# Two tiles on another engine, one buffer more and other planning numbers in a two-layer decoder kernel

## The chip, the core and the metric

The kernel runs on one core of a Trainium2 chip. The metric is device time of one execution in microseconds (us). The time before is 2131.61 us, the median of three runs (2131.43 to 2131.8).

## What is computed

Two layers on x of 1024 tokens by 1024 features, in float32. Layer 0 mixes tokens with a Conformer convolution, layer 1 with sliding-window attention. Each layer then has a layer norm on a scaled residual, a squared-ReLU MLP of inner width 4096, a second norm, and a gated per-layer embedding. Cut to what matters here:

```python
def conformer_conv(x, ...):
    h = x @ w_in + b_in
    a, gate = jnp.split(h, 2, axis=-1)
    h = a * jax.nn.sigmoid(gate)
    h = depthwise_conv(h, w_dw) + b_dw          # 31 taps, causal
    h = jax.nn.silu(layer_norm(h, ln_g, ln_b))
    return h @ w_out + b_out

def swa_sink_attention(x, ...):                 # 16 query heads, 4 key heads, blocks of 128
    scores = where(mask, q @ k / 8, -inf)       # a block sees itself and the block before
    lse = logaddexp(logsumexp(scores), sink)
    return (exp(scores - lse) @ v) @ w_o

def sq_relu_mlp(x, w_up, w_down):
    return jnp.square(jax.nn.relu(x @ w_up)) @ w_down
```

## The kernel before

Each float32 operand is split in two fp32r parts (`wh` and `wl` for weights, `xTh` and `xTl` for the transposed activations), and a product is three matmuls: high by high, high by low, low by high. Larger products use seven half-size products instead of eight, with sums and differences of operands formed on VectorE. PSUM tiles are called `ps` and `tr`.

The order of the work isn't the order of the code. A recorder notes every operation, and a list scheduler (`Recorder.schedule`) then writes one order for all engines: it keeps a planned clock for each engine, takes the duration of each operation from `cost()` (L302) and the planned landing time of a DMA from the table `LANDING` (L87, in ns, by tile name), and issues what can begin first by its rules. A number in these tables therefore moves instructions on every engine and takes no time itself. All instructions come out of one helper, so all stand at line L480 in the profile; tiles have to be told apart by name.

Four places matter here.

- **The convolution's end (taps, 225 to 262 us).** The taps are matmuls `ps<-z,E` of 128x256. Their spread weights `E` are formed on VectorE from `B` (`E<-B,E`), and VectorE also adds tap results together (`A<-A,ps`) and copies transposed pieces out (`A<-tr`). Results go to a DRAM tile `zd` and come back as token rows, `X` (the first 512 features) and `A` (the other 512), as soon as all of a column is written (`X<-zd`, `A<-zd` on SyncE's queue). `conv_ln` (L924) takes BN_STATS of these on VectorE as they land.
- **The norm and what follows (262 to 290 us).** For each half h of the tokens `conv_ln` computes scale and shift (`sm`, with a power on GpSimd), normalises four `X` tiles and four `A` tiles, has TensorE transpose them in groups of four, applies SiLU on ScalarE (`z<-tr` or `z<-ps`), casts the result to `xTh` on ScalarE or VectorE, and forms `xTl` from both on VectorE. `NORM[h][q][f]` (L44) says which engine normalises tile f of X (q = 0) or A (q = 1): v VectorE, a ScalarE, g GpSimd. `CAST[h]` (L45) lists the feature blocks whose cast to `xTh` is ScalarE's; the others are VectorE's. The matmuls of `mix_out` (`ps<-wh,xTh` and so on) wait for these. Matmuls of an embedding projection (`ps<-wh,wh`) are there to fill.
- **The MLP's inner activations.** `mlp()` (L1237) makes the four quarters of a pair of inner tiles; `keep()` (L1076) then forms four sums of them on VectorE, s1 to s4, and stores each to the DRAM tile `hid` by SyncE. s1 and s2 are the two halves of one `zz` tile (one slot), s3 takes the place of a quarter, and s4 is written over s2, once s2's store has read it. `head_forms()` (L1098) does the same for the pairs that were made ahead; both are called after the third pair (m = `HEAD_FORMS` = 2). Later the down product loads these sums back (`wh<-hid`, `raw<-hid`).
- **Attention (1178 to 1345 us).** For each block of 128 queries and four heads, TensorE makes scores (`ps<-E,X`), ScalarE copies one half of them to a `z` tile (`z<-ps`) and VectorE the other by a mask (`COPY_PREDICATED z<-cst,ps`); VectorE takes the negative maximum, ScalarE four exponentials with their sums, VectorE the reciprocal, and GpSimd multiplies each head by it (`TENSOR_SCALAR z<-z,sm`, 128x128). TensorE transposes the four (`ps<-ident,z`), ScalarE and VectorE split them in `A` tiles, GpSimd masks copies of these (`AFFINE_SELECT A<-A`), and TensorE multiplies by the values (`tr<-A,v`, `tr<-A,bo`). Query and output projections fill the gaps.

Of the kernel before, what the change touches and what calls it, by code (L numbers as in the profile page):

```python
# [13 lines left out]
ALU = mybir.AluOpType  # L14
# [7 lines left out]
HT = 512  # L22
# [7 lines left out]
NFF = 4 * D // P  # L30
# [10 lines left out]
LO = 288  # L41
LAG = 8
EMBEDDED = 2
NORM = (("vavg", "vgvg"), ("vgvg", "gggg"))  # L44
CAST = (1, 3, 5, 7), (1, 3, 5, 7)  # L45
DIRECT = 5
BACK = (7, 0, 1)
PLAIN = 2
# [19 lines left out]
HEAD_FORMS, SUMS, FIRST, DEFER = 2, (4, 6), 8, 300  # L68
# [15 lines left out]
    },  # L84
)
CST = 256 + 2 * NH
LANDING = dict(scr=4000.0, qd=5000.0, kd=5000.0, ad=5500.0, zd=4500.0, wsum=5000.0, proj=4500.0, xsp=4000.0, hid=3400.0)  # L87
SLACK = 900.0
LOADED = 1500.0

# [120 lines left out]
class Recorder:  # L211
# [90 lines left out]
    def cost(self, o, outs, allv):  # L302
        e, n = o.eng, o.name
        f = outs[0].n if outs and isinstance(outs[0], View) else 1024
        if e == "tensor":
            if n == "transpose":
                return 113.5
            return f * 0.4427
        if n == "dma_start":
            return 920.0 if e == "gpsimd" else 620.0 if any(v.buf.tag in ("qd", "kd") for v in allv) else 420.0  # L310
        if e == "scalar":
            t = 60.0 + f * 0.85
            if n == "activation":
                t += sum(c for k, c in (("bias", 90.0), ("scale", 130.0), ("accum_out", 110.0)) if isinstance(o.kw.get(k), View))
            return t
        if e == "gpsimd":
            if n == "tensor_tensor":
                return 590.0 if o.kw["op"] == ALU.pow else 60.0 + 3.1 * f
            return 100.0 + 1.95 * f if n == "tensor_scalar" else 160.0 + 0.95 * f
        psum = any(v.buf.space == "PSUM" for v in allv)  # L320
        if n == "tensor_scalar" and not psum:
            return 100.0 + f * 0.69
        if n in ("bn_stats", "tensor_reduce"):
            return 69.0 + 1.042 * allv[-1].n
        if n == "reciprocal":
            return 60.0 + 6.3 * f
        t = 120.0 if isinstance(o.kw.get("scalar"), View) else 70.0
        return t + f * 1.042

    def schedule(self):  # L330
# [45 lines left out]
        def finish(o, end):  # L376
            o.end = end
            order.append(o)
            for x in o.outs:
                r = end + delay(o, x) + (0.0 if o.eng in ("tensor", "alloc") else x.slack)  # L380
                if r > x.ready:
                    x.ready = r
                x.left -= 1
                if x.left == 0:
                    enable(x)
            for b in o.bufs:
                b.users -= 1
                b.end = max(b.end, end)
                if b.users == 0 and b.slot is not None:
                    heapq.heappush(self.tags[b.tag]["free"], (b.end + lat, b.slot))  # L390
                    serve(b.tag)
# [24 lines left out]
        while True:  # L416
# [41 lines left out]
            if o.name == "dma_start":  # L458
                v = o.allv[0]
                dma = max(dma, t + 1400.0) + v.n * v.parts / 75.0  # L460
                names = [x.buf.tag.rstrip("0123456789_") for x in o.allv]
                least = max(LANDING.get(x, 2800.0) for x in names)
                finish(o, max(dma, t + (6500.0 if e == "gpsimd" else least)))
# [49 lines left out]
class Emit:  # L513
# [200 lines left out]
    def conv(self):  # L714
# [209 lines left out]
        def conv_ln(h):  # L924
# [13 lines left out]
            for q in range(2):  # L938
                for f in range(PH):
                    z = Z[h, f, q]  # L940
                    if NORM[h][q][f] == "a":
                        nc.scalar.activation(z, z, AF.Identity, bias=rs[:, f, 1:2], scale=rs[:, f, 0:1])
                        continue
                    e = {"v": nc.vector, "g": nc.gpsimd}[NORM[h][q][f]]
                    e.tensor_scalar(out=z, in0=z, scalar1=rs[:, f, 0:1], scalar2=rs[:, f, 1:2], op0=ALU.mult, op1=ALU.add)
            for k in range(KB):
# [4 lines left out]
                sl = (slice(None), k, slice(h * HT, (h + 1) * HT))  # L951
                if k in CAST[h]:
                    nc.scalar.copy(self.xTh[sl], sv)
# [122 lines left out]
    def keep(self, i, f, c, new=True):  # L1076

        nc = self.nc
        sub, add = ALU.subtract, ALU.add
        w = nc.tile("zz", (P, 1024), F32)  # L1080
        s1, s2 = w[:, 0:HT], w[:, HT : 2 * HT]
        nc.vector.tensor_tensor(out=s1, in0=c[0, 1], in1=c[1, 1], op=add)
        self.store(i, f, "s1", s1)
        if new:
            self.store(i, f, (1, 1), c[1, 1])
        nc.vector.tensor_tensor(out=s2, in0=s1, in1=c[0, 0], op=sub)
        self.store(i, f, "s2", s2)
        s3 = c[0, 1]
        nc.vector.tensor_tensor(out=s3, in0=c[0, 0], in1=s3, op=sub)
        self.store(i, f, "s3", s3)  # L1090
        if new:
            self.store(i, f, (0, 0), c[0, 0])
        nc.vector.tensor_tensor(out=s2, in0=c[1, 0], in1=s2, op=sub)
        self.store(i, f, "s4", s2)
        if new:
            self.store(i, f, (1, 0), c[1, 0])

# [139 lines left out]
    def mlp(self, i):  # L1237
        nc, d, ws = self.nc, self.d, self.ws
        tags, xtags = (dict(zip((2, 1, 3, 4), "XAEB")), "EB") if i == 0 else (dict(zip((2, 1, 3, 4), "XEAB")), "AB")
        first, pairs = list(range(HEAD[i])), list(range(HEAD[i], NFF, 2))  # L1240
        ws.add(*[d["w_up"][i, f] for f in first])
        for f in pairs:
            ws.add(*self.pair_units([d["w_up"][i, f + k] for k in range(2)]))

        us = ws.get(len(first))
        for h in range(2):
            for f in first:
                self.store(i, f, (f % 2, h), self.up(f, h, us[f]))
        ws.done(len(first))

        T = self.token_forms(tags)
        plain = {
            (a, h): [tuple(x[:, k + 4 * a, h * HT : (h + 1) * HT] for x in (self.xTh, self.xTl)) for k in range(4)]
            for a, h in ((0, 0), (1, 0), (1, 1))
        }

        prod = self.half_product

        def copy(ps, tag="t"):
            v = self.sb(tag)  # L1260
            nc.scalar.copy(v, ps)
            return v

        def plus(a, ps):
            nc.vector.tensor_tensor(out=a, in0=a, in1=ps, op=ALU.add)
            return a


        for m, f in enumerate(pairs):
            w = ws.get(1)[0]  # L1270
            p = prod(w, 0, plain[0, 0])
            c11 = copy(p)
            p2 = prod(w, 1, plain[1, 0])
            ws.done(1)
            w12 = ws.get(1)[0]
            prod(w12, 0, T[2], p)
            c21 = copy(p)
            self.square(plus(c11, p2), "z")
            w34 = ws.get(1)[0]
            r = prod(w34, 0, T[3])  # L1280
            prod(w12, 1, T[1], p)
            ws.done(1)
            c22 = copy(p, "bo")
            self.square(plus(c22, r), "z")
            w = ws.get(1)[0]
            prod(w34, 1, plain[1, 1], p)
            c12 = self.square(p, "z")
            prod(w, 0, T[4], r)
            ws.done(2)
            self.square(plus(c21, r), "z")  # L1290
            with nc.later(DEFER if f == pairs[-1] else 0):
                self.keep(i, f, {(0, 0): c11, (0, 1): c12, (1, 0): c21, (1, 1): c22})
            if m == HEAD_FORMS:
                for g in first[::2]:
                    self.head_forms(i, g)
            if m in SUMS:
                self.down_sums(i, SUMS.index(m))
            if f == NFF - FIRST:
                ops = self.first_operands(i)

        self.x = []
        for t in range(NT):
            self.x.append(self.pair(xtags[t // 4]))
        self.begun = set()
        self.turn = 0
        for k in range(3):
            nc.move("tr", "ps")
        for n, cs in enumerate(DOWN):
            self.down_seven(i, cs, None if n else ops, n == len(DOWN) - 1)
# [650 lines left out]
```

## Time and profile before

| | |
|---|---|
| median of three runs | 2131.61 us (2131.43 to 2131.8) |
| profiled execution, time | 2130.39 us |
| its span on the core | 2128.7 us |
| around the span (2130.39 - 2128.7) | 1.7 us |
| granted TensorE clock | 0.999 |
| busy: PE, DVE, ACT, POOL | 99%, 73%, 49%, 10% |

In the profile PE is TensorE, DVE VectorE, ACT ScalarE, POOL GpSimd, SP SyncE. A timeline row has the start in us, the duration in us, the engine, the operation with out<-in, the shape, a count of merged instructions (the duration then runs from the first start to the last end), and in square brackets the idle time just before and what ended it. Matmuls are pipelined, so that the durations of neighbours overlap; the step from start to start says what a matmul costs.

### The profile page before, as it was taken

To read this page: it belongs to the slowest core of one execution; us is meant where nothing else is said; L and a number is where in the kernel's file an instruction comes from. 1 tells how busy PE (TensorE), PEld (TensorE's weight loads), DVE (VectorE), ACT (ScalarE), POOL (GpSimd) and SP (SyncE) were. 2 spreads that over 40 slices of the span, in tenths; PEclk is the share of its full clock that TensorE was granted. 3 is DMA by queue.
4 is the path that set the end of the run, shared out by engine and by line. 5 is a ranking of instruction groups with operands and counts; after the bars stand their busy time and mean duration, and the time that the engine had idled before them with its cause. 6 is when DMAs were issued, how large, how long until landed. Compare 5 with 4: busy or idle time off the path is not lost.

```text
span 2128.7 us, 28513 instructions
## 1 busy us (share of the span) xinstructions
PE 2116.5 (99%) x10067; PEld 1762.7 (83%) x10067; DVE 1562.8 (73%) x2362; ACT 1044.3 (49%) x1886; POOL 206.9 (10%) x390
## 2 busy tenths in 40 slices
PE   9999999999999999999999999999999999999999
PEld 7888888888888888888889877888888888888887
DVE  8766868966666787889554798796665658878993
ACT  7555743555555433341323798365555563333321
POOL 0000141000000200000000566100000011000010
PEclk9999999999999999999999999999999999999999
DMA  7679882347547955530567671354654598445223
GB/s 248 194 205 281 276 216 99 105 168 241 180 167 295 252 183 174 175 127 25 170 193 221 212 234 60 114 195 147 214 197 139 182 332 241 152 159 188 90 70 104
DMA packets 208078, 384.61 MB, mean 181 GB/s; under 512 B 28736, under 2 KB 82496, under 8 KB 207936
## 3 DMA queue, kind: packets, MB, share of 16 engines
q1 hardware_dynamic: 200880, 369.96, 52.2%
q0 software_dynamic: 6912, 12.59, 3.4%
q8 instruction: 79, 1.29, 0.3%
q14 instruction: 63, 0.52, 0.1%
q10 hardware_dynamic: 144, 0.26, 0.0%
HBM read 263.98 MB, written 114.56 MB: 178 GB/s over the span
## 4 chain that ended last, share of the span: by engine, by line
PE 93%; DVE 3%; DMA 1%; ACT 1%; issue 0%; POOL 0%; SPq 0%; DVEq 0%; ACTq 0%; POOLq 0%
PE ps L480 71%; PE tr L480 21%; DMA wh<-hid 1%; DVE xTl L480 1%; DVE sm L480 0%; ACT z L480 0%; DVE wl L480 0%; DVE E L480 0%; DVE B L480 0%; DVE A L480 0%; DVE t L480 0%; DVE z L480 0%; DMA X<-qd 0%; POOL A L480 0%; ACT t L480 0%
## 5 line engine op out<-in xcount | busy, mean ns | idle before, releaser
L480 DVE TENSOR_TENSOR wl<-raw,wh 128x1024 fp32r<-128x1024 f32 (+2 forms) x144 | 151.5, 1053 | 132.8 <-ACT wh L480 132.2
L480 PE MATMUL ps<-xTl,xTh 128*128 128x512 f32 x628 | 244.3, 389 | 0.0
L480 PE MATMUL ps<-xTh,xTl 128*128 128x512 f32 x628 | 244.3, 389 | 0.0
L480 PE MATMUL ps<-xTh 128*128 128x512 f32 x628 | 244.1, 389 | 0.0
L480 PE MATMUL ps<-xTh,wh 128*128 128x512 f32 x608 | 238.8, 393 | 1.1 <-ACT bo L480 0.5
L480 PE MATMUL ps<-xTl,wh 128*128 128x512 f32 x608 | 238.5, 392 | 0.0
L480 PE MATMUL ps<-xTh,wl 128*128 128x512 f32 x608 | 237.6, 391 | 0.0
L480 ACT CAST wh<-raw 128x1024 fp32r<-128x1024 f32 (+2 forms) x144 | 131.2, 913 | 195.7 <-PE ps L480 93.7
L480 DVE TENSOR_TENSOR wl<-g,wh 128x512 fp32r<-128x512 f32 x140 | 92.1, 687 | 97.3 <-ACT wh L480 97.2
L480 PE MATMUL ps<-wl,xTh 128*128 128x512 f32 (+1 forms) x424 | 162.6, 384 | 0.0
L480 PE MATMUL ps<-wh,xTh 128*128 128x512 f32 (+1 forms) x424 | 161.5, 383 | 0.0
L480 PE MATMUL ps<-wh,xTl 128*128 128x512 f32 (+1 forms) x424 | 160.6, 380 | 0.0
L480 ACT CAST wh<-g 128x512 fp32r<-128x512 f32 x140 | 82.8, 621 | 143.7 <-PE ps L480 89.4
L480 ACT CAST xTh<-wh 128x1024 fp32r<-128x1024 f32 x78 | 81.9, 1050 | 126.4 <-PE ps L480 100.6
L480 PEld LDWEIGHTS ps<-xTh,xTl 128*128 128x128 f32 x628 | 117.8, 188 | 24.6
L480 PEld LDWEIGHTS ps<-xTh 128*128 128x128 f32 x628 | 117.9, 188 | 24.5
L480 PEld LDWEIGHTS ps<-xTl,xTh 128*128 128x128 f32 x628 | 117.9, 188 | 24.4
L480 PEld LDWEIGHTS ps<-xTh,wh 128*128 128x128 f32 x608 | 114.3, 188 | 26.7 <-ACT bo L480 1.5
L480 PEld LDWEIGHTS ps<-xTh,wl 128*128 128x128 f32 x608 | 114.4, 188 | 23.5
L480 PEld LDWEIGHTS ps<-xTl,wh 128*128 128x128 f32 x608 | 114.5, 188 | 21.9 <-DVE xTl L480 0.2
L480 DVE TENSOR_TENSOR xTl<-wh,xTh 128x1024 fp32r<-128x1024 f32 x78 | 95.3, 1222 | 27.8 <-ACT xTh L480 27.8
L480 DVE TENSOR_TENSOR xTl<-wl,xTh 128x1024 fp32r<-128x1024 f32 x80 | 97.4, 1220 | 3.7 <-ACT xTh L480 3.7
(316 smaller groups left out, 4962.2 us busy)
## 6 DMA issues: line engine op xcount, KB each, us to landing
wh<-hid SPq DMA_DIRECT2D x80, 512.0 KB, 4.5
raw<-in_w_up_dram SPq DMA_DIRECT2D x64, 512.0 KB, 4.0
wl<-in_w_down_dram SPq DMA_DIRECT2D x60, 512.0 KB, 4.6
hid<-zz SPq DMA_DIRECT2D x96, 256.0 KB, 3.2
hid<-t SPq DMA_DIRECT2D x70, 256.0 KB, 2.7
raw<-hid SPq DMA_DIRECT2D x30, 512.0 KB, 4.5
z<-scr SPq DMA_DIRECT2D x32, 256.0 KB, 3.5
proj<-t SPq DMA_DIRECT2D x32, 256.0 KB, 3.6
```

The costliest lines, as they stand in the source:

```text
L480: getattr(getattr(nc, o.eng), o.name)(*a, **k)
```

## The change

It has six edits.

1. In half 0 the second `A` tile that GpSimd normalised goes to ScalarE (`NORM`, L44).
2. In half 0 the casts to `xTh` on ScalarE are those of blocks 0, 1, 2, 4, 6 in place of 1, 3, 5, 7 (`CAST`, L45).
3. The planned landing time of transfers with `zd` goes from 4500 to 6500 ns, with `hid` from 3400 to 4500 ns (`LANDING`, L87).
4. GpSimd's planned durations change (`cost()`): a power 590 to 560; a tensor_tensor of f elements 60 + 3.1f to 90 + 2.2f; a tensor_scalar of fewer than 512 elements 100 + 1.95f to 160 + 1.17f; the rest 160 + 0.95f to 160 + 1.17f.
5. In `keep()` s4 gets a buffer of its own (a fresh `t` tile; for the pairs made ahead it is written over quarter (1, 0), which isn't needed any longer; for the last pairs over s1) in place of s2's half of `zz`.
6. `head_forms()` is called for one pair after the third pair and for the other after the fourth.

```diff
-NORM = (("vavg", "vgvg"), ("vgvg", "gggg"))
-CAST = (1, 3, 5, 7), (1, 3, 5, 7)
+NORM = (("vavg", "vavg"), ("vgvg", "gggg"))
+CAST = (0, 1, 2, 4, 6), (1, 3, 5, 7)
...
-LANDING = dict(scr=4000.0, qd=5000.0, kd=5000.0, ad=5500.0, zd=4500.0, wsum=5000.0, proj=4500.0, xsp=4000.0, hid=3400.0)
+LANDING = dict(scr=4000.0, qd=5000.0, kd=5000.0, ad=5500.0, zd=6500.0, wsum=5000.0, proj=4500.0, xsp=4000.0, hid=4500.0)
...
             if n == "tensor_tensor":
-                return 590.0 if o.kw["op"] == ALU.pow else 60.0 + 3.1 * f
-            return 100.0 + 1.95 * f if n == "tensor_scalar" else 160.0 + 0.95 * f
+                return 560.0 if o.kw["op"] == ALU.pow else 90.0 + 2.2 * f
+            return 100.0 + 1.95 * f if n == "tensor_scalar" and f >= HT else 160.0 + 1.17 * f
...
-        s3 = c[0, 1]
+        s3, s4 = c[0, 1], c[1, 0] if not new else s1 if f >= NFF - 4 else self.sb("t")
...
-        nc.vector.tensor_tensor(out=s2, in0=c[1, 0], in1=s2, op=sub)
-        self.store(i, f, "s4", s2)
+        nc.vector.tensor_tensor(out=s4, in0=c[1, 0], in1=s2, op=sub)
+        self.store(i, f, "s4", s4)
...
-            if m == HEAD_FORMS:
-                for g in first[::2]:
-                    self.head_forms(i, g)
+            if 0 <= m - HEAD_FORMS < len(first) // 2:
+                self.head_forms(i, first[2 * (m - HEAD_FORMS)])
```

TensorE's order is the same in both programs but for three places: at the end of the taps, between the norm and the output projection of layer 0, and in attention. Three pieces follow.

First, VectorE at the end of the taps. `X_589`, `X_600`, `X_602`, `X_604` and `X_609` are token rows loaded from `zd`; `A_678` and `A_692` are sums of tap results, `E_684` to `E_690` spread weights. Before:

```order
L480 TENSOR_TENSOR A_678_2797<-A_678_2797,ps_657_2682 64x512
L480 TENSOR_TENSOR E_684_2843<-B_653_2658,E_684_2843 128x9x64
L480 BN_STATS sm_64_128<-X_602_2400 128x6
L480 TENSOR_TENSOR E_687_2861<-B_655_2670,E_687_2861 128x9x64
L480 TENSOR_TENSOR E_690_2879<-B_661_2701,E_690_2879 128x9x64
L480 COPY A_579_2312<-tr_670_2765 128x64
L480 BN_STATS sm_65_129<-X_604_2406 128x6
L480 COPY A_594_2372<-tr_670_2765 128x64
L480 BN_STATS sm_68_132<-X_609_2437 128x6
L480 TENSOR_TENSOR A_692_2891<-A_692_2891,ps_680_2815 64x512
```

After the change:

```order
L480 BN_STATS sm_62_126<-X_589_2356 128x6
L480 TENSOR_TENSOR E_687_2859<-B_655_2670,E_687_2859 128x9x64
L480 COPY A_579_2312<-tr_670_2765 128x64
L480 TENSOR_TENSOR E_690_2877<-B_661_2701,E_690_2877 128x9x64
L480 COPY A_594_2372<-tr_670_2765 128x64
L480 BN_STATS sm_63_127<-X_600_2393 128x6
L480 TENSOR_TENSOR A_692_2887<-A_692_2887,ps_680_2815 64x512
```

The statistics have moved back: the sum `A_692`, which frees a PSUM bank, now stands behind those of two X tiles, where it stood behind those of five.

Second, VectorE between the norm's last tiles of half 0 and its first `xTl`. `z_688` is the first SiLU result, `sm_67` the scale and shift of half 1, `X_609` and `X_620` are X tiles of half 1. Before:

```order
L480 TENSOR_TENSOR wl_629_2521<-raw_617_2478,wh_628_2519 128x1024
L480 TENSOR_TENSOR wl_705_2960<-raw_630_2524,wh_706_2964 128x1024
L480 CAST xTh_340<-z_688_2862 128x512
L480 CAST xTh_340<-z_711_2985 128x512
L480 TENSOR_TENSOR xTl_341<-z_688_2862,xTh_340 128x512
L480 TENSOR_TENSOR xTl_341<-z_697_2915,xTh_340 128x512
```

After the change:

```order
L480 TENSOR_TENSOR wl_629_2521<-raw_617_2478,wh_628_2519 128x1024
L480 SCALAR_TENSOR_TENSOR sm_67_131<-sm_66_130,sm_67_131 128x4
L480 TENSOR_TENSOR wl_705_2959<-raw_630_2524,wh_706_2962 128x1024
L480 TENSOR_SCALAR X_609_2437<-X_609_2437,sm_67_131 128x512
L480 TENSOR_SCALAR X_620_2491<-X_620_2491,sm_67_131 128x512
L480 TENSOR_TENSOR xTl_341<-z_688_2860,xTh_340 128x512
L480 TENSOR_TENSOR xTl_341<-z_696_2913,xTh_340 128x512
```

The two casts are gone from here, to ScalarE, and two tiles of half 1 have come in ahead of the first `xTl`.

Third, ScalarE at the same place; `A_592` is the tile that came from GpSimd. After the change:

```order
L480 ACTIVATE X_600_2393<-X_600_2393,sm_61_125 128x512
L480 ACTIVATE A_592_2366<-A_592_2366,sm_61_125 128x512
L480 CAST wh_628_2519<-raw_617_2478 128x1024
L480 CAST wh_706_2962<-raw_630_2524 128x1024
L480 ACTIVATE z_688_2860<-tr_713_3014,cst_337 128x512
L480 ACTIVATE z_696_2913<-ps_722_3068,cst_337 128x512
L480 CAST xTh_340<-z_688_2860 128x512
```

Before, the second of these rows wasn't there, and a third SiLU (`z_711`) stood where the cast of `z_688` stands now. On TensorE the transposes of half 1's X tiles stand earlier than before.

## Prediction

> **What bounds the kernel now.** First the engines' busy share on the page, then TensorE's waits over the whole span, then TensorE's share by stage.
>
> ```profile
> PE 2116.5 (99%) x10067; PEld 1762.7 (83%) x10067; DVE 1562.8 (73%) x2362; ACT 1044.3 (49%) x1886; POOL 206.9 (10%) x390
> ```
>
> ```profile
> PE ps L480 <- DVE t L480: 1.5, 1, 1.5
> PE ps L480 <- POOL z L480: 1.2, 2, 0.7
> PE ps L480 <- DVE z L480: 1.0, 2, 0.8
> PE ps L480 <- issue: 1.0, 1, 1.0
> PE ps L480 <- POOL A L480: 0.8, 1, 0.8
> PE tr L480 <- DVE t L480: 0.7, 3, 0.3
> PE ps L480 <- ACT bo L480: 0.5, 1, 0.5
> PE ps L480 <- ACT xTh L480: 0.5, 1, 0.5
> PE tr L480 <- DVE B L480: 0.2, 1, 0.2
> ```
>
> ```profile
> 310.00:1178.00 868.00, 867.30 (x4020) 722.24 (x4019) 619.27 (x877) 374.59 (x568) 38.99 (x59) 1.00 0.53 173
> 1178.00:1345.00 167.00, 163.81 (x868) 132.01 (x867) 141.75 (x295) 133.28 (x453) 100.62 (x216) 1.00 0.55 172
> 1345.00:2128.70 783.70, 779.29 (x3519) 645.27 (x3518) 570.86 (x809) 348.58 (x520) 31.25 (x48) 1.00 0.50 168
> 800.00:900.00 100.00, 100.00 (x443) 82.81 (x442) 80.02 (x96) 35.49 (x40) 0.00 (x0) 1.00 0.53 174
> ```
>
> In the stage rows the columns are length, busy time of PE, PEld, DVE, ACT, POOL, PE's clock, DMA share, GB/s. TensorE is the bound, at full clock, and its named waits add up to 7.4 us, 1.5 of them at the start. The change adds and removes no matmul. So it can win only what is left of these waits, and lose wherever a reordered helper comes late. From 310 to 1178 TensorE idles 0.7 of 868 us, both of the MLP's products of layer 0 included. The last row gives the unit: 100 us / 443 = 0.226 us per 128x512 matmul. A measurement of this kernel can tell 0.2%, or 4.3 us, from no change.
>
> **Taps (longer `zd` loads).** TensorE's longest wait of this stage, and VectorE's rows that lead to its end; then the load.
>
> ```profile
> 247.48 0.71 PE L480 MATMUL ps<-z,E 128*128 128x256 f32 x4 [1.02 <-issue]
> ```
>
> ```profile
> 240.21 0.69 DVE L480 BATCH_NORM_STATS2 sm<-X 128x6 f32<-128x512 f32 x1 [1.47 <-DMA X<-zd]
> ...
> 243.06 0.69 DVE L480 BATCH_NORM_STATS2 sm<-X 128x6 f32<-128x512 f32 x1
> ...
> 245.97 0.68 DVE L480 BATCH_NORM_STATS2 sm<-X 128x6 f32<-128x512 f32 x1
> 246.69 0.69 DVE L480 TENSOR_TENSOR A<-A,ps 64x512 f32<-64x512 f32 x1
> ```
>
> ```profile
> X<-zd SPq DMA_DIRECT2D x8, 256.0 KB, 6.3
> ```
>
> The matmul at 247.48 needs the bank that the sum at 246.69 frees at 247.38. The sum was late because VectorE stood 1.47 us for a token load that took 6.3 us where 4.5 were planned, and had five statistics of 0.69 ahead of it. With 6.5 planned three of them move behind the sum. Walking VectorE's new order with these durations, the bank is free at about 245.5. But TensorE comes there four matmuls sooner (four of the filling matmuls now stand behind): its own unhindered time is the wait's start 247.48 - 1.02 = 246.46, less 4 x 0.226, so about 245.5. The wait shrinks to 0.1: **gain 0.9**. Bounds: all of it, 1.0; or, if the release stays at 247.38, the four matmuls of cover lost, 0.9 slower.
>
> **Norm (edits 1 and 2).** TensorE, GpSimd (its A tiles by duration, least, median, most), ScalarE and VectorE there:
>
> ```profile
> 268.30 0.33 PE L480 MATMUL ps<-ident,A 128*128 128x128 f32 x1 [0.84 <-POOL A L480]
> 268.46 0.60 PE L480 MATMUL tr<-ident,A 128*128 128x128 f32 x4
> 268.82 0.48 PE L480 MATMUL ps<-wh,xTh 128*128 128x512 f32 x1
> ...
> 270.18 0.48 PE L480 MATMUL ps<-wh,xTl 128*128 128x512 f32 x1
> ```
>
> ```profile
> L480 POOL TENSOR_SCALAR A<-A,sm x6: 769/934/3047, 264.3 to 280.1; 128x512 f32<-128x512 f32 x6
> ```
>
> ```profile
> 264.29 3.95 POOL L480 TENSOR_SCALAR A<-A,sm 128x512 f32<-128x512 f32 x2
> ```
>
> ```profile
> 262.80 0.82 ACT L480 ACTIVATE X<-X,sm 128x512 f32<-128x512 f32 x1 [1.25 <-DVE sm L480]
> 263.53 1.99 ACT L480 CAST wh<-raw 128x1024 fp32r<-128x1024 f32 x2
> 265.41 0.78 ACT L480 ACTIVATE z<-tr,cst 128x512 f32<-128x512 f32 x1
> ...
> 267.41 0.62 ACT L480 CAST xTh<-z 128x512 fp32r<-128x512 f32 x1
> ```
>
> ```profile
> 262.80 1.00 DVE L480 TENSOR_SCALAR X<-X,sm 128x512 f32<-128x512 f32 x2
> ...
> 265.42 2.34 DVE L480 TENSOR_TENSOR wl<-raw,wh 128x1024 fp32r<-128x1024 f32 x2
> 267.69 1.17 DVE L480 CAST xTh<-z 128x512 fp32r<-128x512 f32 x2
> 268.77 2.49 DVE L480 TENSOR_TENSOR xTl<-z,xTh 128x512 fp32r<-128x512 f32 x4
> ```
>
> GpSimd's two A tiles run 264.29 to 268.24, the second 3.05 us under VectorE's `wl`, and TensorE waits 0.84 for it. With one tile on ScalarE the remaining one takes the first's place, is done by about 265.3, and this wait goes. What is late next is ScalarE: the extra tile costs the step 263.53 - 262.80 = 0.73, so the `wh` casts, the first SiLU (now 266.14) and the second come 0.73 later, and the first cast to `xTh`, behind both, starts at 266.14 + 2 x 0.67 = 267.5 and ends at 268.1. TensorE's first `xTh` matmul then starts near 268.15 instead of 268.82; a group of four transposes (0.44) that came before it now comes after, so the gain is 0.67 - 0.44, **0.2**.
>
> Next comes `xTl`. Before, its first was done 0.6 into the row at 268.77, 269.4, and wanted at 270.18. Now VectorE has two X tiles of half 1 ahead of it, after `wl` ends at 267.76 and a small step of 0.15. Their price is unsure: two took 1.00 at 262.80 while GpSimd began beside them, and 1.84 further on:
>
> ```profile
> 274.80 1.84 DVE L480 TENSOR_SCALAR X<-X,sm 128x512 f32<-128x512 f32 x2
> ```
>
> GpSimd has its own tiles of half 1 then, as it had at 274.80, so I take 1.84: `xTl` is done at 267.9 + 1.84 + 0.6 = 270.3. TensorE, with four matmuls (0.9) to do from 268.15, wants it at about 269.1. **Loss 1.2** (0.3 with the cheap price). For the norm that is a net loss of 0.9, bounds 0.1 and 1.3. The X tiles of half 1 that are transposed earlier now have GpSimd's tiles ahead of them; before, nothing waited there, so nothing is won by it.
>
> The Trainium skill, page "SBUF — State Buffer", section "Who interferes with whom", says that a VectorE instruction with two SBUF inputs shuts out a GpSimd instruction that reads SBUF for its whole length, and that whichever comes first blocks the other fully. The 3.05 us under `wl` agree. By that rule alone VectorE's two X tiles would pay a whole GpSimd tile only if that had begun first, and the norm's net could be 0.1 as well as 0.9; the row of 1.84 decides here.
>
> **Attention (edit 4).** GpSimd's groups, with count, busy time and mean ns:
>
> ```profile
> L480 POOL TENSOR_SCALAR z<-z,sm 128x128 f32<-128x128 f32 x125 | 56.5, 465 | 20.1 <-DVE sm L480 18.0 <-ACT z L480 2.0
> L480 POOL TENSOR_SCALAR_AFFINE_SELECT A<-A 128x512 fp32r<-128x512 f32 x56 | 35.8, 641 | 16.8 <-ACT A L480 12.8 <-DVE A L480 3.3
> ```
>
> The planner had 100 + 1.95 x 128 = 350 ns for the first and 160 + 0.95 x 512 = 646 for the second; it now has 310 and 759, further from 465 and 641. No instruction is added; scores, softmax and transposes of the blocks are only set at other distances. TensorE's named waits here are POOL z 1.2, DVE z 1.0 and DVE t 0.7, in all 2.9. Counting matmuls between a block's scores and its first transpose, the distance is as long as before on average, over three us shorter at most, nearly four longer at most. How short it may be is shown by a block that runs without a named wait:
>
> ```profile
> 1314.90 0.52 PE L480 MATMUL ps<-E,X 128*128 128x256 f32 x3
> ...
> 1321.94 0.27 PE L480 MATMUL ps<-ident,z 128*128 128x128 f32 x1
> ```
>
> ```profile
> 1320.94 0.72 POOL L480 TENSOR_SCALAR z<-z,sm 128x128 f32<-128x128 f32 x2 [1.15 <-DVE sm L480]
> ```
>
> Its first normalised head is done at about 1321.3, 6.4 us after its scores. In the new order two blocks fall below this, those transposed before at 1232.7 and 1300.1: 27 matmuls' worth (6.1 us) and 5.8, so short by 0.3 and 0.6. Some eight others lose one to four us of distance but keep 6.7 or more; each is planned 4 x (350 - 310) = 0.16 us shorter by four heads, 1.3 together. That is 2.2 of new waits. Of the 2.9 named ones I let half go, 1.5, since those blocks get longer distances. **Net loss 0.7.** Bounds: 2.6 won, if nearly all named waits go and nothing is late; 6 lost, if the eight blocks are late by 0.7 each and the two by 0.9.
>
> **MLP (edits 3, 5, 6).** The s4 subtraction no longer waits for s2's store; the counts of VectorE's sums and of SyncE's stores are the same, and only local order changes there. TensorE never waits in the up products, so nothing is won; the wait for ACT bo (0.5) stands behind a `wh<-hid` load that is issued at the same place. VectorE's cover is its idle quarter. **0**, bounds 0.4 either way.
>
> **Sum.** -0.9 + 0.9 + 0.7 + 0 = +0.7 on the profiled execution, 2130.39 to 2131.1; the median of the runs is 1.2 above that execution, so 2131.61 + 0.7 = 2132.3.
>
> **Rivals.**
> - *Slower: the softmax chain is too slow for the new distances.* Against 6.4 us of chain the eight shortened blocks keep 6.7 to 8.3, and ScalarE, VectorE and GpSimd are busy 133, 142 and 101 of the 167 us there, so a chain queues longer than that one did. For it: the planner is now 155 ns short per normalisation. Against: the affine selects are planned 118 ns too long, two per block, which gives half of that back. It decides from 0.7 us per block; the price is the bound, 6: 2131.6 - 0.9 + 0.9 + 6 = 2137.6. Chance 0.31.
> - *Faster: the waits simply go.* Taps 1.0, norm only 0.1 lost, attention 2.6, both 0.5 waits for ACT gone, and 0.4 at the MLP: 2131.6 - 4.9 = 2126.7. For it: each named wait has a cause that one of the edits touches. Against: the two ACT waits keep their order. Chance 0.10.
> - *The change does not do what it says.* A wait goes from GpSimd to ScalarE and VectorE at the norm, longer planned loads stand where TensorE never waited: -0.9 + 0.9, attention even, 2131.6, inside the same bound. Chance 0.12.
>
> **How the numbers follow.** My forecast, 2132.3, has 0.47; with the third rival 0.59 lies within 0.2% of before. The range of 8 in 10 goes from 2127.5 (taps, attention and MLP at their good bounds, 1.0 + 2.6 + 0.4) to 2138.0, which takes in the slower rival's price and leaves about one in ten above. Faster 0.10, same 0.59, slower 0.31.
>
> **What would show it.** Taps: TensorE's wait of 1.02 near 247 is gone or a tenth. Norm: no wait for POOL A, but one of about a microsecond for DVE xTl near 269. Attention: waits for POOL z and DVE z of 2 to 4 us in all; over 6, and the slower rival is right. MLP: TensorE still idles under 1 us from 310 to 1178. The forecast falls if the time leaves 2127.3 to 2135.9, or if the waits in attention move it by more than 4 us.

## The result and the profile after

| | before | after |
|---|---|---|
| median of 22 runs each | 2131.04 us (2128.64 to 2135.26) | 2127.05 us (2125.19 to 2128.88) |
| ratio after / before | | 0.9981, 95% interval 0.9974 to 0.9987 |
| profiled execution | 2130.39 us | 2127.52 us |
| its span | 2128.7 us | 2125.8 us |

The change makes the kernel 4.0 us faster (2131.04 - 2127.05), 0.19%. The interval excludes no change. The time lies below the range that was forecast, by half a microsecond, and on the other side of before than the forecast.

The busy line of the page after, and then TensorE's waits over the whole span:

```profile
PE 2115.8 (100%) x10067; PEld 1762.0 (83%) x10067; DVE 1560.1 (73%) x2359; ACT 1046.2 (49%) x1888; POOL 201.1 (9%) x391
```

```profile
PE ps L480 <- DVE t L480: 1.5, 1, 1.5
PE ps L480 <- ACT t L480: 1.2, 2, 0.7
PE ps L480 <- DVE A L480: 0.7, 2, 0.5
PE tr L480 <- ACT z L480: 0.7, 1, 0.7
PE ps L480 <- DVE xTl L480: 0.4, 1, 0.4
PE ps L480 <- ACT xTh L480: 0.3, 1, 0.3
PE tr L480 <- DVE t L480: 0.2, 1, 0.2
```

The waits for POOL z, DVE z and POOL A are gone. Others have come: ACT z and DVE xTl at the norm, ACT t and DVE A in the MLP and behind attention. The named waits fell from 7.4 to 5.0 us.

Waits by name don't say where the time came from, but the same work in both traces does. TensorE executes 10067 matmuls in both, and outside the three places of the change in the same order. So the n-th matmul of one trace is the n-th of the other, and the stretch between two such matmuls is the time of a stage with all its waits, named or not. By stretches, from the first matmul to the last, with the marks in the time of before:

| stretch of before (us) | before | after | difference |
|---|---|---|---|
| 0 to 240, start and convolution | 238.58 | 238.30 | -0.28 |
| 240 to 262, end of the taps | 22.11 | 21.06 | -1.05 |
| 262 to 295, norm | 33.02 | 33.47 | +0.45 |
| 295 to 425, output projection and norm | 129.91 | 129.91 | 0 |
| 425 to 560, up product of layer 0 | 134.87 | 135.87 | +1.00 |
| 560 to 1178, down product and the rest of layer 0 | 618.21 | 617.18 | -1.03 |
| 1178 to 1345, attention | 166.83 | 163.47 | -3.36 |
| 1345 to 1440, projection behind it | 95.03 | 95.93 | +0.90 |
| 1440 to 1700, up product of layer 1 | 260.14 | 260.82 | +0.68 |
| 1700 to the end | 423.98 | 423.81 | -0.17 |

Attention is the largest row. One can see it in plain windows too: in the same 163 us TensorE gets through 851 matmuls before

```profile
1178.00:1341.00 163.00, 159.81 (x851) 128.68 (x850) 139.19 (x292) 132.23 (x452) 100.62 (x216) 1.00 0.55 173
```

and 866 after:

```profile
1178.00:1341.00 163.00, 162.40 (x866) 131.13 (x865) 139.56 (x293) 132.99 (x452) 96.14 (x216) 1.00 0.57 176
```

That is 15 more, at 0.226 us for one of 128x512 3.4 us. But the busy time in these rows has risen by 2.6 only. A 128x512 matmul is shown 0.39 us long, and the next can start 0.23 behind its start. So the first 0.16 us of a stall count as busy, and a wait is named 0.16 shorter than what it costs, or not at all. The 0.65 us that are named at 555.9 us in the trace after (the row stands below), for instance, belong to a step that is 0.81 too long.

The end of the taps, TensorE and VectorE after:

```profile
245.27 0.84 PE L480 MATMUL ps<-z,E 128*128 128x256 f32 x5
```

```profile
240.05 0.69 DVE L480 TENSOR_TENSOR A<-A,ps 64x512 f32<-64x512 f32 x1 [0.97 <-ACT A L480]
...
243.77 0.68 DVE L480 BATCH_NORM_STATS2 sm<-X 128x6 f32<-128x512 f32 x1
244.48 0.69 DVE L480 TENSOR_TENSOR A<-A,ps 64x512 f32<-64x512 f32 x1
```

VectorE doesn't stand for a token load any more, the sum that frees the bank ends at 245.17 in place of 247.38, and TensorE has no named wait there (the step before it is 0.3 us too long).

The norm after, TensorE, ScalarE, VectorE, GpSimd. Everything there happens 1.34 us earlier than before (the first ScalarE tile is at 261.46, was at 262.80):

```profile
265.60 0.66 PE L480 MATMUL tr<-ident,X 128*128 128x128 f32 x4 [0.73 <-ACT z L480]
266.26 0.66 PE L480 MATMUL ps<-ident,A 128*128 128x128 f32 x4
266.77 0.50 PE L480 MATMUL ps<-wh,xTh 128*128 128x512 f32 x1
...
268.35 0.50 PE L480 MATMUL ps<-wh,xTl 128*128 128x512 f32 x1 [0.37 <-DVE xTl L480]
```

```profile
262.18 0.80 ACT L480 ACTIVATE A<-A,sm 128x512 f32<-128x512 f32 x1
262.89 1.98 ACT L480 CAST wh<-raw 128x1024 fp32r<-128x1024 f32 x2
264.77 0.77 ACT L480 ACTIVATE z<-tr,cst 128x512 f32<-128x512 f32 x1
```

```profile
266.41 1.29 DVE L480 TENSOR_SCALAR X<-X,sm 128x512 f32<-128x512 f32 x2
267.62 1.27 DVE L480 TENSOR_TENSOR xTl<-z,xTh 128x512 fp32r<-128x512 f32 x2
```

```profile
265.46 3.92 POOL L480 TENSOR_SCALAR X<-X,sm 128x512 f32<-128x512 f32 x2 [0.43 <-DVE sm L480]
```

The wait for GpSimd's A tile is gone, and in its place TensorE waits 0.73 for the SiLU that the extra ScalarE tile pushed back, and 0.37 for the first `xTl`, which stands on VectorE behind two X tiles of half 1.

### The profile page after: what moved, and what is told of

It is laid out like the page before. It is cut to its first block, busy times and chain, and to the rows that moved or that the text cites. A ratio compares the mean times of both kernels' runs of the same rounds, so it can differ in the third digit from the quotient of the medians.

```text
span 2125.8 us, 28547 instructions
## 1 busy us (share of the span) xinstructions
PE 2115.8 (100%) x10067; PEld 1762.0 (83%) x10067; DVE 1560.1 (73%) x2359; ACT 1046.2 (49%) x1888; POOL 201.1 (9%) x391
## 3 DMA queue, kind: packets, MB, share of 16 engines
q8 instruction: 79, 1.29, 0.2%
## 4 chain that ended last, share of the span: by engine, by line
PE 95%; DVE 2%; DMA 2%; ACT 1%; issue 0%; POOL 0%; SPq 0%; DVEq 0%; ACTq 0%; POOLq 0%
PE ps L480 73%; PE tr L480 22%; DMA raw<-in_w_up_dram 1%; DVE A L480 1%; DVE wl L480 0%; DMA wh<-hid 0%; ACT z L480 0%; DVE sm L480 0%; DMA X<-in_xT_dram 0%; ACT t L480 0%; DVE t L480 0%; ACT wh L480 0%; DVE xTl L480 0%; POOL sm L480 0%; SPq L480 0%
## 5 line engine op out<-in xcount | busy, mean ns | idle before, releaser
L480 DVE TENSOR_TENSOR xTl<-wl,xTh 128x1024 fp32r<-128x1024 f32 x80 | 97.3, 1218 | 3.4 <-ACT xTh L480 3.4
```

The lines of the kernel that those rows point to most:

```text
L480: getattr(getattr(nc, o.eng), o.name)(*a, **k)
```

## The experiments

Besides times, each run was read by the stretches above. Attention and norm repeat to 0.3 us or better wherever the program has the same order, so that one execution tells there; taps and up product don't repeat so well. All in one table, in us; the last column says whose order TensorE has in attention.

| run | taps | norm | up product 0 | attention | order in attention |
|---|---|---|---|---|---|
| before | 22.11 | 33.02 | 134.87 | 166.83 | before |
| after | 21.06 | 33.47 | 135.87 | 163.47 | after |
| e1_gps | 22.01 | 33.03 | 137.36 | 163.54 | after |
| e3_norm | 21.53 | 33.49 | 136.86 | 166.92 | before |
| e4_zd | 21.10 | 33.05 | 135.98 | 166.89 | before |
| e5_mlp | 21.11 | 33.02 | 135.14 | 167.08 | before |
| e6_aff | 21.15 | 33.01 | 136.00 | 164.06 | a new one |
| e7_ts | 21.15 | 33.03 | 136.29 | 164.80 | a new one |
| e10_nudge | 21.54 | 33.01 | 135.52 | 165.01 | a new one |
| e13_nudge_down | 21.67 | 33.01 | 135.83 | 164.70 | a new one |
| e8_cal | 21.53 | 33.04 | 136.72 | 165.62 | a new one |
| e11_s4 | 21.24 | 33.01 | 135.93 | 166.98 | before |
| e12_hid_head | 21.77 | 33.02 | 134.67 | 166.86 | before |
| e9_nonorm | 21.05 | 33.01 | 135.27 | 163.48 | after |

Single executions, whose time alone says little: e6_aff 2128.78, e7_ts 2126.9, e10_nudge 2127.18 and e11_s4 2129.4 beside 2127.92 of before on the same chip, e8_cal 2130.22, e13_nudge_down 2128.65 and e12_hid_head 2128.4 beside 2132.32 of before (median of 9).

### One edit at a time

**GpSimd's planned durations alone.**

```diff
-                return 590.0 if o.kw["op"] == ALU.pow else 60.0 + 3.1 * f
-            return 100.0 + 1.95 * f if n == "tensor_scalar" else 160.0 + 0.95 * f
+                return 560.0 if o.kw["op"] == ALU.pow else 90.0 + 2.2 * f
+            return 100.0 + 1.95 * f if n == "tensor_scalar" and f >= HT else 160.0 + 1.17 * f
```

> The kernel before with edit 4 alone (GpSimd's planned durations). Theory A: the gain of the change comes out of attention and is this edit's; TensorE's work from the 1178.2 us mark to the 1345.0 mark of before, 166.8 us there and 163.5 in the changed kernel, takes 163.5 +- 0.5 here, and the time is 3.4 us below before (ratio 0.9984). Theory B: the attention gain needs the earlier edits too (they shift what is in flight when attention begins); 165.5 or more here, at most 1.5 us below before.

Measured: attention 163.54, the changed kernel's 163.47. Theory A holds: attention's gain is this edit's, and needs no other. Time 2129.07 (11 runs) against 2130.97 (33 runs), ratio 0.999, interval 0.9981 to 0.9999. That is 1.9 us less where 3.4 were expected; the interval takes in both.

**Second A tile to ScalarE and the casts, alone.**

```diff
-NORM = (("vavg", "vgvg"), ("vgvg", "gggg"))
-CAST = (1, 3, 5, 7), (1, 3, 5, 7)
+NORM = (("vavg", "vavg"), ("vgvg", "gggg"))
+CAST = (0, 1, 2, 4, 6), (1, 3, 5, 7)
```

> The kernel before with edits 1 and 2 alone (NORM and CAST of half 0). Theory A: TensorE's stretch from the 262.2 us mark to the 295.2 mark of before, 33.0 us there and 33.5 in the changed kernel, takes 33.4 to 33.6: a loss of 0.5 us, the time within 1 us of before. Theory B: the 0.45 us of loss comes from the taps' tail that ends a microsecond earlier in the changed kernel, so that loads are late at the norm; then 33.0 or less here, no loss.

Measured: norm 33.49 against 33.01 to 33.05 in all runs without these edits. Ratio 1.0007, interval 0.9999 to 1.0016. The two edits lose 0.46 us whatever the taps do; the time alone couldn't have told it.

**Longer planned landing of `zd`, alone.**

```diff
-LANDING = dict(..., zd=4500.0, ...)
+LANDING = dict(..., zd=6500.0, ...)
```

> The kernel before with the longer planned landing of zd alone (edit 3, first half). Theory A: the taps' stretch from the 240.1 us mark to the 262.2 mark of before, 22.1 us there and 21.1 in the changed kernel, takes 21.1 +- 0.15; the norm's stretch after it stays at 33.0; the time is 1 us below before. Theory B: the gain there is chance of the one execution (the token load lands early or late); then anything from 21.1 to 22.1, and no difference in the time.

Measured: taps 21.10; ratio 0.9997, interval 0.9988 to 1.0006. The table decides between the theories, and both have a part. The three runs with 6500 take 21.05 to 21.10. The eleven with 4500 take anything from 21.11 to 22.11, 21.53 in the mean, because it hangs on when the token load lands: where VectorE waits 0.4 us for the load the stretch is 21.11 (e5_mlp), at 0.9 it is 21.53 (e3_norm), at 1.5 it is 22.11, and with 6500 VectorE waits for no load there. The profile of before happened to be the worst of them. The edit is worth about 0.45 us (21.53 - 21.07), not the 1.05 that the two profiles show.

**s4's buffer, head_forms and planned `hid`, alone.**

```diff
-LANDING = dict(..., hid=3400.0)
+LANDING = dict(..., hid=4500.0)
...
-        s3 = c[0, 1]
+        s3, s4 = c[0, 1], c[1, 0] if not new else s1 if f >= NFF - 4 else self.sb("t")
...
-        nc.vector.tensor_tensor(out=s2, in0=c[1, 0], in1=s2, op=sub)
-        self.store(i, f, "s4", s2)
+        nc.vector.tensor_tensor(out=s4, in0=c[1, 0], in1=s2, op=sub)
+        self.store(i, f, "s4", s4)
...
-            if m == HEAD_FORMS:
-                for g in first[::2]:
-                    self.head_forms(i, g)
+            if 0 <= m - HEAD_FORMS < len(first) // 2:
+                self.head_forms(i, first[2 * (m - HEAD_FORMS)])
```

> The kernel before with edit 5 (s4's own buffer), edit 6 and the longer planned landing of hid alone. TensorE's order is that of before everywhere. Theory A: these are worth nothing; the two waits of 0.8 and 0.7 us that the changed kernel shows at 555.9 and 1599.0 us are the chance of weight loads that landed late in that execution; here the time is within 1 us of before, and such waits appear at other places or not at all. Theory B: the stores of s4 now come right behind a weight load and delay it; the two waits appear here at the same two places with 0.5 to 1 us each, and the time is 1 to 2 us above before.

Measured: ratio 0.9994, interval 0.9985 to 1.0003 (2129.89 against 2130.97), which doesn't exclude no change; TensorE's step at the place of 555.9 is 0.2 us too long, that of 1599.0 is not. Theory B falls: such waits stand at 556 in e1_gps, e3_norm, e7_ts and e13_nudge_down too (0.8 to 1.1 us), which have the old `keep()`. Theory A is not the whole truth either, as the traces of the other runs showed: with the old `keep()` there is a wait near 525 us that the profile of before didn't have. Before, VectorE and SyncE there:

```profile
521.07 0.69 DVE L480 TENSOR_TENSOR zz<-z,bo 128x512 f32<-128x512 f32 x1 [0.98 <-DVE g L480]
...
524.22 0.68 DVE L480 TENSOR_TENSOR bo<-bo,ps 128x512 f32<-128x512 f32 x1
```

```profile
517.11 0.32 SPq L480 DMA_DIRECT2D hid<-zz  x1
```

And in e1_gps, which has the same order there, VectorE, SyncE and TensorE:

```profile
523.81 0.69 DVE L480 TENSOR_TENSOR zz<-z,bo 128x512 f32<-128x512 f32 x1 [2.77 <-issue]
...
526.95 0.68 DVE L480 TENSOR_TENSOR bo<-bo,ps 128x512 f32<-128x512 f32 x1
```

```profile
518.06 0.32 SPq L480 DMA_DIRECT2D hid<-zz  x1
```

```profile
527.68 0.50 PE L480 MATMUL ps<-B,wh 128*128 128x512 f32 x1 [1.30 <-DVE bo L480]
```

The sum s1 of the next pair needs the one `zz` slot, in which s4 of the pair before is being stored. From the store's issue to the sum it took 4.0 us before and 5.8 us in e1_gps; 3.4 were planned. Behind the sum on VectorE stand `wl` and `bo<-bo,ps`, and TensorE needs that last one. VectorE stood 1.0 us before and TensorE not at all; 2.8 and 1.5 (its step's excess, 1.30 of it named) in e1_gps. The names given for VectorE's wait (DVE g, long done, and "issue") hide the store. Over the nine executions with old `keep()`, head_forms and `hid`, TensorE's excess at this place is 0, 0, 0.6, 0.7, 0.75, 1.1, 1.1, 1.5 and 1.7, in the mean 0.8 us; over the five with any of these edits it is 0 each time. The whole stretch agrees: 136.2 in the mean of those nine and 135.4 of the five, though single ones go from 134.9 to 137.4 and from 134.7 to 135.9.

**Which of the three it is.** s4's own buffer alone:

```diff
-        s3 = c[0, 1]
+        s3, s4 = c[0, 1], c[1, 0] if not new else s1 if f >= NFF - 4 else self.sb("t")
...
-        nc.vector.tensor_tensor(out=s2, in0=c[1, 0], in1=s2, op=sub)
-        self.store(i, f, "s4", s2)
+        nc.vector.tensor_tensor(out=s4, in0=c[1, 0], in1=s2, op=sub)
+        self.store(i, f, "s4", s4)
```

> The kernel before with edit 5 alone (s4 in its own buffer). In four executions with the old keep VectorE stands 1.0, 1.5, 2.0 and 2.8 us near 521 us of the run for the one zz slot, whose s4 is still being stored, and TensorE then 0, 0.7, 1.1 and 1.5 us for the sum (bo<-bo,ps) behind it on VectorE; with edits 3 to 6 this wait is not there. Theory A: s4's own buffer alone removes it: VectorE waits 0.3 us or less for zz there and TensorE not at all. Theory B: it was the other order (head_forms spread, longer planned hid) that took the sum away from there; then VectorE still stands 1 us or more at the same place here.

Measured: the sum is no longer at this place, VectorE waits for no `zz`, TensorE has no wait at 525; but its step at 517.3 is 0.7 too long, for a copy to a `t` tile by ScalarE, which was held by another store. Theory A's forecast came out at that place, and in this one execution as much was lost next to it. But the sum has moved, so the order changed together with the slot.

Spread head_forms and longer `hid` alone, without the buffer:

```diff
-LANDING = dict(..., hid=3400.0)
+LANDING = dict(..., hid=4500.0)
...
-            if m == HEAD_FORMS:
-                for g in first[::2]:
-                    self.head_forms(i, g)
+            if 0 <= m - HEAD_FORMS < len(first) // 2:
+                self.head_forms(i, first[2 * (m - HEAD_FORMS)])
```

> The kernel before with the longer planned landing of hid and edit 6 (head_forms spread), without s4's own buffer. Theory A (the one zz slot, held until s4 is stored, is what VectorE waits for): the wait for zz is still there, at 521 us or where the sum now stands, 1 us or more on VectorE. Theory B (the order is what counts): the sum has moved away from TensorE's tight place near 525 us and TensorE doesn't wait for bo there, though VectorE may still wait for zz.

Measured: up product 134.67, the lowest of all; no wait at 525; the `zz` sums stand elsewhere on VectorE. There they wait for the store of a former one 0.7 us in all by the named waits, and TensorE doesn't wait for them. So either half is enough to clear this place, and Theory B is right that a new order does it with the one slot kept. That the slot alone does it isn't shown, since the sum moved in both runs. How the 0.8 us divides stays open: with single executions of a stretch that spreads by over two us it can't be told.

### Why attention gains

The affine selects alone (759 ns in the plan in place of 646):

```diff
-            return 100.0 + 1.95 * f if n == "tensor_scalar" else 160.0 + 0.95 * f
+            return 100.0 + 1.95 * f if n == "tensor_scalar" else 160.0 + 1.17 * f
```

> The kernel before with only one of GpSimd's planned durations changed: the affine selects (and copies) 160 + 0.95f to 160 + 1.17f, 646 to 759 ns for 512 elements. TensorE's attention stretch is 166.8 to 167.1 us in four executions with the old durations and 163.5 in two with all of edit 4. Theory A (slack: the longer plan for the selects gives the values matmuls room): 164.2 or less. Theory B (a draw: edit 4 only deals the order anew, and the order of before was a poor one): any value from 163 to 168, unrelated to the direction of the change. Theory C (accuracy, the one of the prediction: 759 is further from the measured 641): 166.8 or more.

The normalisations alone (310 ns in place of 350):

```diff
-            return 100.0 + 1.95 * f if n == "tensor_scalar" else 160.0 + 0.95 * f
+            return 100.0 + 1.95 * f if n == "tensor_scalar" and f >= HT else 160.0 + 1.17 * f if n == "tensor_scalar" else 160.0 + 0.95 * f
```

> The kernel before with only the normalisations' planned duration changed: tensor_scalar of 128 elements 350 to 310 ns, where they take 465 in the mean. Theory A (slack by the affine selects): no gain, 166.5 or more in attention. Theory B (a draw): any value from 163 to 168. Theory C (accuracy: 310 is further from 465): slower than before, 167.5 or more.

A nudge of 5 ns:

```diff
-            return 100.0 + 1.95 * f if n == "tensor_scalar" else 160.0 + 0.95 * f
+            return (100.0 + 1.95 * f if f >= HT else 100.0 + 1.95 * f) if n == "tensor_scalar" else 165.0 + 0.95 * f
```

> The kernel before with all of GpSimd's other planned durations (affine selects and copies) 5 ns longer, 165 + 0.95f: a nudge of under one per cent with no meaning. TensorE's order in attention is a new one all the same. Theory A (slack) and theory C (accuracy): attention stays at 166.8 +- 0.5. Theory B (a draw): it moves by a microsecond or more, either way.

Measured: 164.06, 164.80 and 165.01. The first would suit the slack theory, but a nudge with no meaning wins 1.8 us, more than half of the whole. The theory of slack and that of accuracy fall. TensorE's waits in attention of e10_nudge:

```profile
PE ps L480 <- POOL z L480: 1.1, 2, 0.7
PE tr L480 <- DVE t L480: 0.2, 1, 0.2
PE ps L480 <- issue: 0.2, 1, 0.2
```

Its first wait for POOL z, at 1218 us, is that of before. From 1228 us of before on the order is another, and the waits for DVE z and most of those for DVE t don't come.

Two more draws were to say whether the side of the change matters, the nudge in the other direction and the plan at the measured duration:

```diff
-            return 100.0 + 1.95 * f if n == "tensor_scalar" else 160.0 + 0.95 * f
+            return (100.0 + 1.95 * f if f >= HT else 100.0 + 1.95 * f) if n == "tensor_scalar" else 155.0 + 0.95 * f
```

> The kernel before with GpSimd's other planned durations 5 ns shorter, 155 + 0.95f, the opposite of the nudge that took attention from 166.8 to 165.0. Theory B (a draw): attention moves by a microsecond or more against before or stays within 0.5, and not by the mirror image; any value from 163 to 168. A theory of slack (longer plans for the selects are what helps): 167.5 or more.

```diff
-            return 100.0 + 1.95 * f if n == "tensor_scalar" else 160.0 + 0.95 * f
+            return (100.0 + 1.95 * f if f >= HT else 340.0 + 0.98 * f) if n == "tensor_scalar" else 160.0 + 0.95 * f
```

> The kernel before with the normalisations planned at what they take in its own profile, 465 ns for 128 elements in place of 350 (340 + 0.98f); the affine selects stay at 646, where 641 were measured. Theory B (a draw): attention, 166.8 us before, takes anything from 163 to 168. Theory C (accuracy, the one of the prediction): this is the best of the plans, 163.5 or less. A third theory (pessimism: a longer plan sets the transposes further back, TensorE waits less for them but the block chain gets longer and the end of attention drains): 166 or more.

Measured: 164.70 with 5 ns less, so the two nudges move it the same way; 165.62 with the measured duration, the least gain of all. Its waits are of other kinds:

```profile
PE ps L480 <- ACT t L480: 0.5, 1, 0.5
PE tr L480 <- DVE t L480: 0.4, 2, 0.3
PE ps L480 <- DVE z L480: 0.4, 1, 0.4
PE ps L480 <- DVE A L480: 0.3, 1, 0.3
```

Seven orders of attention give 163.5, 164.1, 164.7, 164.8, 165.0, 165.6 and 166.8. That of before is the worst, that of the change the best, and the direction or the accuracy of the plan doesn't sort them. Of the three theories only B, the draw, fits all of them: the edit deals the order anew. That all six new orders are better than that of before says that before had a poor one, as e6_aff's theory B put it, and not that new numbers help. What makes a single order good wasn't tried further.

### Without the edits that lose

The changed kernel with `NORM` and `CAST` as before:

```diff
-NORM = (("vavg", "vavg"), ("vgvg", "gggg"))
-CAST = (0, 1, 2, 4, 6), (1, 3, 5, 7)
+NORM = (("vavg", "vgvg"), ("vgvg", "gggg"))
+CAST = (1, 3, 5, 7), (1, 3, 5, 7)
```

> The changed kernel without edits 1 and 2: the second A tile back on GpSimd, the casts as before. If the stages add up, the norm's stretch takes 33.0 us in place of 33.5, taps 21.1, attention 163.5, and the time is 0.5 us below the changed kernel's, 4.5 us below before (ratio 0.9979, which the interval can't tell from the changed kernel's 0.9981). The rival: the edits hang together and the norm waits 33.4 or more here too.

Measured: norm 33.01, taps 21.05, attention 163.48: the stages add up. Time 2124.74 (5 runs) against 2132.32 (9 runs), ratio 0.9963, interval 0.995 to 0.9977. That overlaps the changed kernel's interval by a little (0.9974 to 0.9987), so the times alone don't rank the two for sure; the norm's stretch does, by 0.46 us. The time is 7.6 us below before where 4.5 were expected, and the interval, 4.9 to 10.7 us, leaves that out. Before took longer in this round (2132.32) than in the 22 runs of the result (2131.04), and the waits at 555.9, 1599.0 and behind attention, about 2 us in the profile after, are absent from this one; whether that is chance stays open. Its waits:

```profile
PE ps L480 <- DVE t L480: 1.5, 1, 1.5
PE ps L480 <- POOL A L480: 0.8, 1, 0.8
PE ps L480 <- ACT xTh L480: 0.5, 1, 0.5
PE tr L480 <- DVE t L480: 0.2, 1, 0.2
```

## Why the prediction was wrong, point by point

- **What bounds the kernel: right.** TensorE's stalls moved, and its matmuls are as many as before.
- **Taps, -0.9: right in mechanism and size for this execution** (-1.05), and wrong in what it stood for. The stretch of before spreads from 21.1 to 22.1, and the edit brings it to its good end; in the mean that is 0.45.
- **Norm, +0.9: right in mechanism, half in size (+0.46).** The wait went from GpSimd to ScalarE and VectorE as said. TensorE's first `xTh` matmul is at 266.77 + 1.34 = 268.11, 268.15 was worked out. Two X tiles on VectorE cost 1.29, between the two rows that were shown (1.00 and 1.84); the dearer one had been taken. The two terms, 1.2 lost and 0.2 won, make 1.0 and not 0.9; with 1.29 for 1.84 they make 0.45. The wait for `xTl` is 0.37, not about a microsecond.
- **Attention, +0.7 with -2.6 as its good bound: the step that failed.** It measured -3.4, beyond the bound. The term put 2.2 us of new waits behind the shortened blocks and let go 1.5 of the 2.9 named ones. After the change no transpose of the `z` tiles has a named wait, 0.2 of named waits is left in the stage, and so 2.7 of them went. Two things in the step were wrong. The bound was drawn from the named waits, which leave out 0.16 us of each stall and all that is shorter: at the median steps in this stage, 0.231 us for 128x512, 0.119 for 128x256 and 0.11 for 128x128, its 506, 216 and 144 matmuls need 158.4 us, so that its steps held about 8 us more before and about 5 after. And the sign came from the thought that a plan further from the measured durations makes later chains, by 0.16 us for each of eight blocks. The runs show no such relation: the plan at the measured duration was the least good of six changes, and 5 ns either way won two us. The block chain of 6.4 us was no proof either: the blocks that were to fall short of it didn't cost TensorE a named wait. Why not wasn't traced; the order of all helpers had changed as well.
- **The slower rival** rested on the same chain, and the waits it needed didn't come. Besides, two selects of 118 ns give back 236 of four times 155 = 620 ns, less than the half that it says.
- **MLP, 0 within 0.4: by the traces too small, though the times don't show it.** TensorE idles 0.7 us from 310 to 1178, under 1 as forecast. But "TensorE never waits in the up products" was true of one execution. Nine with the same program there waited 0.8 us in the mean at one place, and edits 3, 5 and 6 clear it. The waits that stand there in the profile after (at 555.9 and 1599.0 us) come in runs with and without the edits:

```profile
555.91 0.73 PE L480 MATMUL ps<-A,wh 128*128 128x512 f32 x2 [0.65 <-ACT t L480]
```

```profile
552.31 0.69 DVE L480 TENSOR_TENSOR g<-raw 128x512 f32<-128x512 f32 x1 [2.25 <-DMA raw<-in_w_up_dram]
```

  Here a weight load landed late, 7.6 us after its issue where the same load took 5.5 in the profile of before, and ScalarE's copy came late behind the casts that wait for it.
- **The sum.** By the stretches: -3.4 for attention, +0.46 norm, -0.45 taps, -0.8 up product, together -4.2, against -4.0 measured. The last two are means over few executions, and the measured gain is known as 2.8 to 5.5 us only, so the agreement is closer than the data can warrant. By their times the four runs with a part of the change each (e1_gps, e3_norm, e4_zd, e5_mlp) give -1.9, +1.1, -1.0 and -1.1, together -2.9, each with an interval about 4 us wide. The rival "the waits simply go" had the right side and with 2126.7 nearly the time, at a chance of one in ten. Part of that is luck: it had 2.6 for attention, 0.1 lost at the norm, 1.0 at the taps, 1.0 for the two waits for ACT and 0.4 in the MLP, and its too small attention and too large taps and ACT make up for each other.

## What to carry to other kernels

Where a list scheduler sets the order, a change of its numbers is first of all a new draw: before arguing from the new number, nudge it by a meaningless amount and see how far the stage moves. Bound a gain by the stretch of the same work, not by the sum of named waits. And a place without a wait in one profile isn't a place without waits: look for a helper that stands behind a store or load with one slot, and ask what is left of its cover when that transfer takes two us longer.

## What the runs showed of the hardware

The same 256 KB store of s4, issued at the same place, was waited for 4.0 us after its issue in one execution and 5.8 in another. The 22 executions of before spread over 6.6 us (2128.64 to 2135.26), those after the change, which takes such waits away, over 3.7 us (2125.19 to 2128.88). That the stores are the reason for the wider spread is likely, but not shown.

Two 128x512 normalisations of X on VectorE took 1.00 us, 1.29 and 1.84 at three places with GpSimd at work on its own tiles. The Trainium skill, page "SBUF — State Buffer", section "Who interferes with whom", has the later of two contending instructions blocked for the whole of the other. At 266.41 a GpSimd tile had been under way since 265.46 and ran to 267.42. VectorE's first tile ended at 266.95 all the same, after 0.54 us, and the second took 0.84, so that the pair lost 0.3 us and didn't stand until the GpSimd tile was done. Before, GpSimd's second A tile had begun at 265.21, ahead of VectorE's `wl` at 265.42, and yet it was GpSimd that was held, to 268.24, and `wl` took 1.21 us a piece, as it did with GpSimd idle (1.22 at 548.51). So the 3.05 us agree with the page in who shuts out whom, but not in that the first comer blocks the other. What exactly was blocked wasn't tried.
